# A feed-forward block's second product by sevens: operand loads apart from their splits, the residual in quarter pieces, the last product half by half

## The chip, the core and the metric

The kernel runs on one core of a Trainium2 chip. Times are microseconds of that core; the figure for a kernel is the median of its runs. Beside it stands one execution under the hardware profiler, from which every row below is taken. In the profile's names PE is TensorE's matmuls and PEld its weight loads, DVE is VectorE, ACT ScalarE, POOL GpSimd, and SP SyncE, the engine that issues nearly all DMAs here. L165 is line 165 of the kernel.

## What is computed

One layer of a decoder trunk on 1024 new tokens of a prompt and 8 x 8 sample tokens, all in fp32: a half-step feed-forward block, a token mixer (pooling branch and state-space branch), a second feed-forward block, a last norm. The change lies in the feed-forward block, which runs twice:

```python
def swiglu(x, w_in, w_out):
    gu = x @ w_in                                   # (tokens, 1024) @ (1024, 2 * 2816)
    g, u = gu[..., :D_FF], gu[..., D_FF:]
    return (jax.nn.silu(g) * u) @ w_out             # (tokens, 2816) @ (2816, 1024)

x = x + 0.5 * swiglu(rmsnorm(x, norm_ffn1), ffn1_w_in, ffn1_w_out)
x = x + mixer(rmsnorm(x, norm_mix), ...)
x = x + 0.5 * swiglu(rmsnorm(x, norm_ffn2), ffn2_w_in, ffn2_w_out)
y = rmsnorm(x, norm_final)
```

## The kernel before

**Layout.** Activations lie with channels on the 128 partitions and tokens along a row. The tokens are cut into two halves h of 512 and 576 (576 includes the 64 sample tokens); each half again into two token groups of NPAIR = 256 or 288, `f` and `s_` in the code. An fp32 matrix is multiplied as two parts, a rounded one and the rest: `split` (lines 354 to 360) makes the rounded part on ScalarE (L356) and the rest on VectorE (L358), and three matmuls take the place of one: weight part `wh` with operand parts `hh` and `hr`, weight part `wl` with `hh`. All matmuls are recorded at line 165, all transposes at 169.

**By sevens.** Both products of a feed-forward block use the scheme that multiplies 2 x 2 blocks with seven products instead of eight, from sums of blocks. In the first product (`ffn_in`, over 22 blocks `ff` of 128 hidden channels) `hidden(h, ff, g)` (L683) takes each finished block `g`. Blocks in pairs, even and odd, and the two token groups are the 2 x 2 blocks of the second product's operand: products 1, 2 and 3 use three of them as they are, 5, 6, 7 and 4 differences, which `sums` computes on POOL (L702). Each of the seven operands is stored by a DMA (L689) to DRAM as `hblock["1"]` to `["7"]`, 11 blocks of 128 x 544 each: 256 columns of half 0 and 288 of half 1.

**The second product** (`second`, L708) takes the seven in the order 1 2 5 6 4 7 3. A product has four *units* m, one for each 128 output channels of a half of the 1024; a unit has 11 steps k (in three chunks of 4, 4 and 3), each of three matmuls for each half: 66 matmuls, accumulated in PSUM banks `po`, one for each half (`unit`, L776). `weights` (L749) loads the raw weight block of a chunk (`raw`, L733, a ring of 6 tiles), for 5, 6 and 7 makes a sum or difference of two on POOL (L757, L761, L766; the sums of 5 are held in 12 tiles `ws`, turned into those of 6 in place and by `fourth`, L774, into those of 3), and `parts` (L739) makes `wh` on ScalarE (L745) and `wl` on VectorE (L746) in rings of 3 each. `leave` (L790) adds half of the unit's result to the output tiles on VectorE (L795).

- Operand blocks: `load_X(p)` (L719) loads one block and emits its split at once. Blocks 0 to 3 lie in 8 `pair` tiles (for product 1 in the pool `fx`), later ones in two tiles of the pool `act`, which has 42 and serves nearly everything. During a product the next one's first 8 blocks are loaded, 0, 3, 3 and 2 after its units (L839); the other three stand at the next product's start (L826).
- Residual: in product 7 each unit loads four whole tiles of the old x from DRAM (`xo`, L835) and after its `leave` adds them on POOL (L821, 512 or 576 columns each).
- The last product, 3: units 0 and 1 for both halves, then units 2 and 3 for half 0, `after(0)`, then units 2 and 3 for half 1, `after(1)`. What `after` starts is the norm that the next stage needs (the mixer, or the last norm with its transposes and the output).
- Before `second` the differences of all blocks, `hsums`, are finished (L671).

**Order.** Work is emitted in the order of the code, and side work (norms, differences, squares) as generators ("chains") that `tick` steps between groups of matmuls, when an estimate of TensorE's time has passed the step's due time: `H_AT` and `H_PACE` (L46) are that delay and pace for the differences. The tile framework then places the instructions of each engine's queue itself: the order of the code is their priority (`high_priority` lifts it), and an instruction goes as soon as the framework's own clock has its inputs ready and its tiles free. In the trace the first load of product 1 stands at 279.8 us, long ahead of `second`. On the chip each queue then runs strictly in the order made.

Of the kernel before, what the change touches and what calls it, by code (L numbers as in the profile page):

```python
# [8 lines left out]
F32 = mybir.dt.float32  # L9
# [5 lines left out]
P = 128  # L15
# [30 lines left out]
H_AT, H_PACE = 4.0, 1.5  # L46
# [17 lines left out]
def tile_hybrid_pool_ssd_macaron(  # L64
# [586 lines left out]
    def ffn(wi, wo, prep, after, half, side=None):  # L651
# [19 lines left out]
        while hsums:  # L671
            finish(hsums.pop(0))
# [10 lines left out]
    def hidden(h, ff, g):  # L683

        n, i, at = NPAIR[h], ff // 2, HALF_AT[h]
# [5 lines left out]
        if ff % 2 == 0:  # L691
            even[h] = g
            put("1", g[:, f])
            return
# [12 lines left out]

    def second(wo, after, half):  # L708
# [7 lines left out]
        xo = {}  # L716
        held = {}

        def load_X(p):  # L719
            k = len(X[p])  # L720
            if k >= 4:
                a, r = act((P, 576), F32R, "hh"), act((P, 576), name="hr")
            elif p == "1":
                a, r = fx(F32R, "hh"), fx(name="hr")
            else:
                a, r, _ = pair(576, "hp")
                r = r.bitcast(F32)
            a, r = a[:, :N2], r[:, :N2]
            dma(r, hblock[p][k])
            split(r, a, r.bitcast(F32R))  # L730
            X[p].append((a, r.bitcast(F32R)))
# [7 lines left out]
        def parts(a, nk, own):  # L739
            if own:  # L740
                wh, wl = (act((P, 4 * P), F32R, t)[:, : nk * P] for t in ("wh", "wl"))
            else:
                wh, wl = (sp.tile([P, 4 * P], F32R, tag=t, bufs=N_W, name=nm(t))[:, : nk * P] for t in ("wh", "wl"))
            with tc.high_priority(hp[0]):
                S.activation(wh, a, AF.Copy)  # L745
                V.tensor_tensor(wl, a, wh.bitcast(F32), op=ALU.subtract)  # L746
            return wh.rearrange("p (k c) -> p k c", c=P), wl.rearrange("p (k c) -> p k c", c=P)

        def weights(p, m, own=False):  # L749
            for kb, nk in chunks:  # L750
                if p in "124":
# [10 lines left out]
                elif p == "7":  # L762
# [4 lines left out]
                else:  # L767
                    a = held.pop((m, kb))
                yield (kb, nk) + parts(a, nk, own)
# [20 lines left out]
        def leave(p, m, h, pt):  # L790
# [20 lines left out]
            elif p == "6":  # L811
                add(a[:, s_], b[:, s_])
                add(b[:, f], t)
            elif p == "4":
                add(b[:, f], b[:, f])
            elif p == "7":
                add(b[:, f], b[:, f])
                add(b[:, s_], a[:, s_])
                for q in (4 + m, m):
                    o = xo.pop((h, q))  # L820
                    G.tensor_tensor(xt[h][q][:, : 2 * n], xt[h][q][:, : 2 * n], o, op=ALU.add)  # L821
            else:
                add(a[:, s_], a[:, s_])

        for p, nxt in zip(order, order[1:] + " "):
            while len(X[p]) < NK2:  # L826
                load_X(p)
            if p == "3":
                break
            for m in range(4):  # L830
                if p == "7":
                    for h in HALVES:
                        for q in (4 + m, m):
                            o = xo[h, q] = act((P, 576), name="xo")[:, : NTOK[h]]
                            dma(o, xspill[h][q])  # L835
# [16 lines left out]
        for h in HALVES:  # L852
            for m in (2, 3):
# [1075 lines left out]
```

## Time and profile before

| | us |
|---|---|
| median of 3 runs (2996.34 to 3004.19) | 2999.07 |
| the profiled execution, as timed | 2992.67 |
| its span in the profile | 2990.9 |
| mean granted clock of TensorE | 0.977 |
| matmuls of the second product, first block | 559.87 to 832.07 |
| matmuls of the second product, second block | 2699.36 to 2975.48 |

How to read it: the span runs from the first instruction to the last; 1.8 us of the timed execution lie around it. A row of the table of windows gives for a stretch of the span its length, the busy time and the instructions (x) of PE, PEld, DVE, ACT and POOL, the clock that TensorE was granted (1.00 is full), the mean busy share of the 16 DMA engines and GB/s. A row of a timeline gives start, length, engine, line, operation, the tile written and the tiles read (`<-`), and in brackets the idle time of the engine before it with what ended it. A row of a group gives the count, the busy time, the mean length in ns, then the idle time before its instructions and what ended it. "SPq" are issues of DMAs.

### The profile page before, as it was taken

To read this page: it belongs to the slowest core of one execution; us is meant where nothing else is said; L and a number is where in the kernel's file an instruction comes from. 1 tells how busy PE (TensorE), PEld (TensorE's weight loads), DVE (VectorE), ACT (ScalarE), POOL (GpSimd) and SP (SyncE) were. 2 spreads that over 40 slices of the span, in tenths; PEclk is the share of its full clock that TensorE was granted. 3 is DMA by queue.
4 is the path that set the end of the run, shared out by engine and by line. 5 is a ranking of instruction groups with operands and counts; after the bars stand their busy time and mean duration, and the time that the engine had idled before them with its cause. 6 is when DMAs were issued, how large, how long until landed. Compare 5 with 4: busy or idle time off the path is not lost. (4 is left out here: it accounts for less than half of the span.)

```text
span 2990.9 us, 54693 instructions
## 1 busy us (share of the span) xinstructions
PE 2813.4 (94%) x19834; PEld 2624.2 (88%) x19834; DVE 1859.9 (62%) x2848; ACT 1400.5 (47%) x3086; POOL 1345.7 (45%) x1392
## 2 busy tenths in 40 slices
PE   7889999999889999999998999898999999998987
PEld 6888899899869999999997887677999999988987
DVE  6655555666685376867675767866665555554746
ACT  5444443533344465555545656566233444344323
POOL 5645666343452264645632233323135665561533
PEclk9999999999999999999999999999999999999999
DMA  4566543576635545553357577786674332335773
GB/s 133 155 214 201 168 137 99 172 228 182 219 88 148 168 157 186 165 172 121 106 195 220 181 217 240 246 259 191 227 252 145 100 110 92 101 116 173 232 223 112
DMA packets 562255, 512.49 MB, mean 171 GB/s; under 512 B 39348, under 2 KB 426792, under 8 KB 561976
## 3 DMA queue, kind: packets, MB, share of 16 engines
q1 hardware_dynamic: 561968, 508.99, 54.4%
q8 instruction: 156, 2.56, 0.4%
q14 instruction: 115, 0.94, 0.1%
q10 hardware_dynamic: 16, 0.00, 0.0%
HBM read 361.28 MB, written 147.80 MB: 170 GB/s over the span
## 5 line engine op out<-in xcount | busy, mean ns | idle before, releaser
L165 PE MATMUL pw<-X,wh 128*128 128x288 f32 (+2 forms) x2832 | 632.2, 312 | 9.6 <-ACT v L565 8.3
L165 PEld LDWEIGHTS pw<-X,wh 128*128 128x128 f32 x2832 | 465.6, 191 | 32.9 <-ACT v L565 9.4
L165 PE MATMUL pw<-X,wl 128*128 128x288 f32 (+1 forms) x1644 | 475.8, 289 | 0.9 <-DVE wl L449 0.9
L449 DVE TENSOR_TENSOR wl<-s,wh 128x512 fp32r<-128x512 f32 x288 | 252.3, 876 | 282.0 <-ACT wh L448 260.9
L165 PE MATMUL pw<-hl,wh 128*128 128x256 f32 (+1 forms) x1536 | 392.0, 328 | 3.3 <-DVE t L569 3.0
L165 PE MATMUL pw<-hi,wh 128*128 128x288 f32 x1120 | 331.3, 296 | 2.6 <-ACT t L601 1.3
L165 PE MATMUL pw<-hi,wl 128*128 128x288 f32 x1120 | 330.2, 295 | 0.8 <-DVE wl L449 0.8
L165 PE MATMUL pw<-lo,wh 128*128 128x288 f32 x1120 | 329.7, 294 | 0.0
L442 POOL TENSOR_TENSOR s<-wraw,wraw 128x512 f32<-128x512 f32 x144 | 196.2, 1362 | 280.5 <-DVE wl L449 209.2
L165 PEld LDWEIGHTS pw<-X,wl 128*128 128x128 f32 x1644 | 314.1, 191 | 1.5 <-DVE wl L449 1.5
L165 PE MATMUL pw<-hl,wl 128*128 128x256 f32 x1072 | 300.3, 280 | 0.0
L165 PEld LDWEIGHTS pw<-hl,wh 128*128 128x128 f32 x1536 | 258.8, 189 | 24.4 <-DVE t L569 3.3
L448 ACT ACTIVATE wh<-s 128x512 fp32r<-128x512 f32 x288 | 181.0, 629 | 155.1 <-PE pw L165 130.6
L449 DVE TENSOR_TENSOR wl<-wraw,wh 128x512 fp32r<-128x512 f32 x216 | 174.9, 811 | 110.6 <-ACT wh L448 101.5
L165 PEld LDWEIGHTS pw<-hi,wh 128*128 128x128 f32 x1120 | 210.5, 188 | 9.8 <-ACT t L601 2.0
L165 PEld LDWEIGHTS pw<-hi,wl 128*128 128x128 f32 x1120 | 210.1, 188 | 1.4 <-DVE wl L449 1.3
L165 PEld LDWEIGHTS pw<-lo,wh 128*128 128x128 f32 x1120 | 210.6, 188 | 0.0
L165 PE MATMUL po<-hh,wh 128*128 128x256 f32 (+1 forms) x848 | 186.3, 296 | 20.2 <-ACT hh L356 10.2
L165 PEld LDWEIGHTS pw<-hl,wl 128*128 128x128 f32 x1072 | 203.0, 189 | 0.0
L448 ACT ACTIVATE wh<-wraw 128x512 fp32r<-128x512 f32 x216 | 135.5, 627 | 141.0 <-PE pw L165 121.5
L165 PE MATMUL po<-hh,wl 128*128 128x256 f32 (+1 forms) x848 | 185.4, 295 | 7.3 <-DVE wl L746 7.0
L165 PE MATMUL po<-hr,wh 128*128 128x256 f32 (+1 forms) x848 | 185.0, 295 | 1.1 <-DVE hr L358 1.0
(396 smaller groups left out, 6817.0 us busy)
## 6 DMA issues: line engine op xcount, KB each, us to landing
wraw<-in_ffn_w_in_dram SPq DMA_DIRECT2D x188, 256.0 KB
wraw<-in_ffn_w_out_dram SPq DMA_DIRECT2D x144, 256.0 KB
wraw<-in_w_in_dram SPq DMA_DIRECT2D x144, 256.0 KB
wh<-part SPq DMA_DIRECT2D x116, 256.0 KB
wl<-part SPq DMA_DIRECT2D x116, 256.0 KB
hr<-hb SPq DMA_DIRECT2D x106, 272.0 KB
hb<-g SPq DMA_DIRECT2D x154, 144.0 KB
hb<-g SPq DMA_DIRECT2D x154, 128.0 KB
```

Of the source, the lines that this page charges most:

```text
L165: T.matmul(out, lhsT, rhs, start=start, stop=stop, skip_group_check=free)
L442: G.tensor_tensor(t, a, b, op=op)
L448: S.activation(wh, a, AF.Copy)
L449: V.tensor_tensor(wl, a, wh.bitcast(F32), op=ALU.subtract)
```

## The change

- `H_AT, H_PACE` go from 4.0, 1.5 to 0.3, 0.3: the differences of a pair of blocks are emitted right behind it.
- `hidden` is cut in two. For the very last block, `hidden_odd` (stores of operands 2 and 3, differences, stores of 5, 6, 7, 4) is put in `hlast` for both halves; `second` first emits all loads and splits of operand 1, then these, then the rest of `hsums`.
- `load_X` becomes `fetch_X(p, n)`, which only issues n loads, and `split_X(below)`, which emits the splits of what has been fetched: at the last chunk of each unit of both halves, and (for blocks under 8) at a product's start. After each unit up to 3 blocks of the next product are fetched, until `AHEAD` of them are there: 11 of products 2 and 5, 8 of 6 and 4, 10 of 7 and 3; the others at the next product's start.
- Residual: of the output tiles' four quarters three are loaded by `old` in pieces of 256 and 288 columns (the first in product 6, two in 7) and added on POOL after the unit; the fourth is loaded by DMA straight into its place in product 6 and the sum that belongs there is added on POOL in product 4.
- Product 3 runs units 0 to 3 for half 0, `after(0)`, units 0 to 3 for half 1, `after(1)`. All 12 pairs of weight parts are kept from one half to the other: unit 0's in the rings `wh` and `wl`, unit 1's in the raw ring and `act`, those of 2 and 3 in `act` (15 tiles of it).

```diff
@@ -43,7 +43,8 @@
...
-H_AT, H_PACE = 4.0, 1.5
+H_AT, H_PACE = 0.3, 0.3
+AHEAD = {'2': 11, '5': 11, '6': 8, '4': 8, '7': 10, '3': 10}
...
@@ -668,8 +669,6 @@
                 ffn_in(wi, ff, [(h, X[h])])
         if side:
             finish(side)
-        while hsums:
-            finish(hsums.pop(0))
         second(wo, after, half)
...
     def hidden(h, ff, g):
 
+        if ff == NFF - 1:
+            hlast.append(lambda: hidden_odd(h, ff, g))
+        elif ff % 2:
+            hidden_odd(h, ff, g)
+        else:
+            even[h] = g
+            n, at = NPAIR[h], HALF_AT[h]
+            dma(hblock["1"][ff // 2][:, at : at + n], g[:, :n])
+
+    def hidden_odd(h, ff, g):
+
         n, i, at = NPAIR[h], ff // 2, HALF_AT[h]
         f, s_ = slice(0, n), slice(n, 2 * n)
 
         def put(p, x):
             dma(hblock[p][i][:, at : at + n], x)
 
-        if ff % 2 == 0:
-            even[h] = g
-            put("1", g[:, f])
-            return
         e = even[h]
         put("2", g[:, f])
         put("3", g[:, s_])
@@ -705,6 +711,8 @@
 
         hsums.append(start(sums(), H_AT))
...
+    hlast = []
+
     def second(wo, after, half):
...
+        raws, held, late_ = [], {}, []
+
+        def fetch_X(p, n):
+            for k in range(len(X[p]), min(len(X[p]) + n, NK2)):
+                if k >= 4:
+                    a, r = act((P, 576), F32R, "hh"), act((P, 576), name="hr")
+                elif p == "1":
+                    a, r = fx(F32R, "hh"), fx(name="hr")
+                else:
+                    a, r, _ = pair(576, "hp")
+                    r = r.bitcast(F32)
+                a, r = a[:, :N2], r[:, :N2]
+                dma(r, hblock[p][k])
+                raws.append((k, r, a))
+                X[p].append((a, r.bitcast(F32R)))
+
+        def split_X(below=NK2):
+            while raws and raws[0][0] < below:
+                _, r, a = raws.pop(0)
+                split(r, a, r.bitcast(F32R))
...
@@ -736,18 +748,26 @@
...
+        def ring(tag, nk):
+            n = {"wraw": N_RAW, "wh": N_W, "wl": N_W}[tag]
+            if tag == "wraw":
+                return sp.tile([P, 4 * P], F32, tag=tag, bufs=n, name=nm("wh")).bitcast(F32R)[:, : nk * P]
+            return sp.tile([P, 4 * P], F32R, tag=tag, bufs=n, name=nm(tag))[:, : nk * P]
+
...
-        def weights(p, m, own=False):
+        def weights(p, m):
             for kb, nk in chunks:
+                if p == "3":
+                    a = held.pop((m, kb))
+                    wh = act((P, 4 * P), F32R, "wh")[:, : nk * P] if m > 1 else ring(("wh", "wraw")[m], nk)
+                    wl = act((P, 4 * P), F32R, "wl")[:, : nk * P] if m else ring("wl", nk)
+                    yield (kb, nk) + parts(a, nk, wh, wl)
+                    continue
...
-                    a = held.pop((m, kb))
-                yield (kb, nk) + parts(a, nk, own)
+                yield (kb, nk) + parts(a, nk, ring("wh", nk), ring("wl", nk))
...
+        def old(m, q, col):
+            t = act((P, 576), name="xo")
+            for h in HALVES:
+                n, at = NPAIR[h], HALF_AT[h]
+                dma(t[:, at : at + n], xspill[h][4 * q + m][:, col * n : (col + 1) * n])
+
+            def put():
+                for h in HALVES:
+                    n, at = NPAIR[h], HALF_AT[h]
+                    o = xt[h][4 * q + m][:, col * n : (col + 1) * n]
+                    G.tensor_tensor(o, o, t[:, at : at + n], op=ALU.add)
+
+            late_.append(put)
+
         def unit(p, m, hs, ws):
             pts = [psum("pd", "po" + p)[:, : NPAIR[h]] for h in hs]
             for kb, nk, wh, wl in ws:
+                if kb == 8 and len(hs) == 2:
+                    split_X()
                 for kk in range(nk):
                     k = kb + kk
                     for j, (W_, lo_) in enumerate(((wh, 0), (wh, 1), (wl, 0))):
...
             elif p == "6":
                 add(a[:, s_], b[:, s_])
                 add(b[:, f], t)
+                dma(b[:, s_], xspill[h][4 + m][:, s_])
             elif p == "4":
                 add(b[:, f], b[:, f])
+                G.tensor_tensor(b[:, s_], b[:, s_], a[:, s_], op=ALU.add)
             elif p == "7":
                 add(b[:, f], b[:, f])
-                add(b[:, s_], a[:, s_])
-                for q in (4 + m, m):
-                    o = xo.pop((h, q))
-                    G.tensor_tensor(xt[h][q][:, : 2 * n], xt[h][q][:, : 2 * n], o, op=ALU.add)
+                add(b[:, s_], b[:, s_])
             else:
                 add(a[:, s_], a[:, s_])
...
-        for p, nxt in zip(order, order[1:] + " "):
-            while len(X[p]) < NK2:
-                load_X(p)
-            if p == "3":
-                break
+        fetch_X("1", NK2)
+        split_X()
+        while hlast:
+            hlast.pop(0)()
+        while hsums:
+            finish(hsums.pop(0))
+        for p, nxt in zip(order[:-1], order[1:]):
+            split_X(8)
+            fetch_X(p, NK2)
             for m in range(4):
-                if p == "7":
-                    for h in HALVES:
-                        for q in (4 + m, m):
-                            o = xo[h, q] = act((P, 576), name="xo")[:, : NTOK[h]]
-                            dma(o, xspill[h][q])
+                if p == "6":
+                    old(m, 0, 0)
+                elif p == "7":
+                    old(m, 1, 0)
+                    old(m, 0, 1)
                 unit(p, m, HALVES, weights(p, m))
                 if p == "4":
                     fourth(m)
-                for _ in range((0, 3, 3, 2)[m]):
-                    load_X(nxt)
+                while late_:
+                    late_.pop(0)()
+                n = AHEAD[nxt] - len(X[nxt])
+                fetch_X(nxt, min(n, 3))
+        fetch_X("3", NK2)
+        split_X()
         for h in HALVES:
             half(h, xt[h])
-        for m in (0, 1):
-            unit("3", m, HALVES, weights("3", m))
-        kept = {m: [] for m in (2, 3)}
+        kept = {m: [] for m in range(4)}
 
         def keep(m):
-            for w in weights("3", m, own=m == 3):
+            for w in weights("3", m):
                 kept[m].append(w)
                 yield w
 
         for h in HALVES:
-            for m in (2, 3):
+            for m in range(4):
                 unit("3", m, [h], kept[m] if h else keep(m))
             after(h, xt[h])
```

More of the change, by code (lines that the diff above doesn't have):

```diff
@@ L737, in raw, with parts @@
             return t
[L739 to L743, printed above, removed]
+        def ring(tag, nk):
[3 more added lines that the diff above has]
+            return sp.tile([P, 4 * P], F32R, tag=tag, bufs=n, name=nm(tag))[:, : nk * P]
+        def parts(a, nk, wh, wl):
             with tc.high_priority(hp[0]):
@@ L761, in weights @@
                         G.tensor_tensor(a, a, x, op=ALU.subtract)
-                elif p == "7":
+                else:
                     a = stage["p"].tile([P, 4 * P], F32, tag="wsum", bufs=N_S, name=nm("ws"))[:, : nk * P]
```

16 lines of the change are left out of this document (removed).

## The prediction

> **What bounds the kernel now.** I read the page first, for the share of TensorE, then the table of busy time by windows, with the edges set where the matmuls into `po` (line 165) change product: 66 matmuls are a unit, four units a product, in the order 1 2 5 6 4 7 3.
>
> ```profile
> span 2990.9 us, 54693 instructions
> PE 2813.4 (94%) x19834; PEld 2624.2 (88%) x19834; DVE 1859.9 (62%) x2848; ACT 1400.5 (47%) x3086; POOL 1345.7 (45%) x1392
> ```
>
> ```profile
> 559.87:599.80 39.93, 36.47 (x266) 35.20 (x265) 17.42 (x26) 15.93 (x32) 4.14 (x4) 0.91 0.58 174
> 599.80:639.04 39.24, 33.72 (x266) 33.06 (x264) 20.14 (x33) 16.71 (x30) 3.87 (x3) 1.00 0.69 206
> 639.04:673.63 34.59, 34.59 (x264) 34.59 (x265) 26.44 (x28) 12.85 (x22) 27.77 (x19) 0.95 0.91 260
> 673.63:709.33 35.70, 33.80 (x267) 33.15 (x265) 28.52 (x43) 14.45 (x26) 8.82 (x6) 1.00 0.58 172
> 709.33:745.75 36.42, 34.23 (x267) 33.31 (x265) 18.94 (x29) 10.13 (x18) 14.63 (x11) 1.00 0.64 186
> 745.75:791.25 45.50, 37.28 (x266) 35.38 (x265) 24.44 (x35) 11.20 (x20) 27.89 (x22) 0.92 0.87 277
> 791.25:832.07 40.82, 36.66 (x278) 35.98 (x276) 26.52 (x41) 16.90 (x30) 9.75 (x8) 0.96 0.44 137
> ```
>
> ```profile
> 2699.36:2739.57 40.21, 36.66 (x267) 35.38 (x266) 17.17 (x26) 15.70 (x31) 3.69 (x4) 0.92 0.56 172
> 2739.57:2780.60 41.03, 34.25 (x267) 33.14 (x265) 20.70 (x35) 16.64 (x30) 4.42 (x3) 0.98 0.63 195
> 2780.60:2816.09 35.49, 35.49 (x265) 35.49 (x266) 26.48 (x27) 12.80 (x22) 28.44 (x19) 0.92 0.89 259
> 2816.09:2851.45 35.36, 33.78 (x266) 33.15 (x265) 28.63 (x43) 14.39 (x26) 8.57 (x6) 1.00 0.57 171
> 2851.45:2886.39 34.94, 33.77 (x267) 33.21 (x265) 17.81 (x28) 10.13 (x18) 14.21 (x11) 1.00 0.66 197
> 2886.39:2931.21 44.82, 37.06 (x267) 35.39 (x265) 23.69 (x34) 11.09 (x20) 28.01 (x22) 0.92 0.79 244
> 2931.21:2975.48 44.27, 41.23 (x320) 40.54 (x319) 28.80 (x45) 19.11 (x44) 10.52 (x8) 0.96 0.10 32
> ```
>
> ```profile
> 2714.80:2739.57 24.77, 24.77 (x201) 24.77 (x200) 8.67 (x14) 9.28 (x20) 0.00 (x0) 1.00 0.37 112
> ```
>
> The columns are stretch, length, busy time of PE, PEld, DVE, ACT and POOL, granted clock, DMA share and GB/s. The last row is three units without a wait: 24.77 / 3 = 8.26 us a unit, 33.0 a product, 231.2 for seven. The two phases last 272.2 and 276.1 us, so 41 + 45 = 86 us are lost in them; this, and what follows the first phase, is all that the change can win. The losses by product: 1: 6.9 and 7.2; 2: 6.2 and 8.0; 5: 1.6 and 2.5; 6: 2.7 and 2.3; 4: 3.4 and 1.9; 7: 12.5 and 11.8; 3: 7.8 and 11.3 (part of it matmuls of others: 278 and 320 instead of 264). The view of the tile `po` says what ended its waits:
>
> ```profile
>   ACT wh L745: 44.9, 18
>   DVE wl L746: 33.9, 38
>   ACT hh L356: 22.6, 18
> ```
>
> So TensorE waits for ScalarE and VectorE, which are half idle. The timelines of ScalarE and SyncE at the start of product 7 show why:
>
> ```profile
> 2886.61 0.63 ACT L745 ACTIVATE wh<-ws 128x512 fp32r<-128x512 f32 x1 [1.93 <-POOL ws L766]
> 2895.78 0.66 ACT L356 ACTIVATE hp<-hp 128x544 fp32r<-128x544 f32 x1 [8.54 <-DMA hp<-hb]
> ```
>
> ```profile
> 2890.37 0.48 SPq L729 DMA_DIRECT2D hp<-hb  x1
> 2890.89 3.67 SPq L835 DMA_DIRECT2D xo<-xspill  x6
> 2894.68 1.41 SPq L729 DMA_DIRECT2D hp<-hb  x2
> ```
>
> ScalarE stands 8.54 us in front of the split of a block that the *next* product needs; that load and six residual loads share the queue. Behind it stand the weight parts that TensorE needs now. Queues are in order, so an early operand split blocks a late weight.
>
> **The change, part by part.** Each term is what of a loss goes.
>
> *Start of product 1 (14.1 lost).*
>
> ```profile
> 2701.11 0.80 SPq L689 DMA_DIRECT2D hb<-g  x2
> 2701.96 0.92 SPq L729 DMA_DIRECT2D hr<-hb  x2
> 2703.48 0.51 PE L165 MATMUL po<-hh,wh 128*128 128x256 f32 x2 [2.23 <-ACT hh L356]
> ```
>
> The two last loads of operand 1 stand on SP behind stores of the last hidden block, which wait for its product on POOL; TensorE then idles, and the product's granted clock is 0.91. The change emits all eleven loads and splits ahead of those stores (`hlast`); what is moved back, twelve stores on SP and eight subtractions on POOL a phase, is read 33 us later, by product 2 or after. Bounds 0 (the loads wait for their tiles anyway) to 14; I take 11, near the upper end, because the row names the store.
>
> *Products 2 and 5 (18.3 lost).*
>
> ```profile
> 2773.90 0.66 ACT L356 ACTIVATE hh<-hr 128x544 fp32r<-128x544 f32 x1 [2.92 <-DMA hr<-hb]
> 2779.93 1.55 ACT L745 ACTIVATE wh<-ws 128x512 fp32r<-128x512 f32 x3
> ```
>
> Splits of operand 5 and 6 come between 2773.90 and 2779.93, each behind its own DMA, and the first weights of product 5 after them. In the code of before each load past the fourth draws its tile after the tile of the split before it, so loads and splits take turns; now three loads go out together, a unit earlier, all eleven of operands 2 and 5 before their product, and the splits stand at the last chunk of the next unit, some 6 us behind. Bounds 0 to 17; I take 12, two thirds, because the six splits of the row's stretch do not vanish but only stop waiting.
>
> *Products 6 and 4 (10.3 lost).* Eight blocks ahead as before, the last three at the product's start. I take 3.5 (0 to 7), for the earlier unit. What they get in addition, a quarter of the residual each on POOL and 0.28 MB more loads a unit in product 6, goes beside a DMA share of 0.58 and 8.8 us of POOL in 35.7: nothing, and rival C if that cover fails.
>
> *Product 7 (24.3 lost).*
>
> ```profile
> 2904.42 5.64 POOL L821 TENSOR_TENSOR x<-x,xo 128x512 f32<-128x512 f32 x4 [8.55 <-DVE x L795]
> ```
>
> Four residual additions take 5.64 us of POOL a unit, after the unit's last matmul and ahead of the next unit's weight sums. By bytes (shapes of the code, four to an element) product 7 moves now 24 raw weight blocks (5.8 MB), some 11 operand blocks of 128 x 544 (3.1) and all the residual (16 loads, 4.5): 13.4 MB, less six raws that fit in their ring beforehand (1.5), at the row's 277 GB/s 43 us for 33 us of matmuls. That is the product's length; the DMA queue sets it, with POOL close behind. The change brings half of the residual during 6 and leaves the other half here: 5.8 + 2.8 + 2.2 - 1.5 = 9.3 MB, 34 us. POOL's additions of a unit fall from 5.64 us to four of half the size, 3.6 us (0.9 each, the row of L702 below), and only two of these wait for the unit. Bounds 5 (the ScalarE wait stays) to 22; I take 15.
>
> *Product 3 (19.1 lost).* POOL reaches it with less behind it, and ten of eleven blocks are fetched; I take 6. Half by half, the first four units need three weight parts in 3.9 us each (33 x 24.77/198 x 256/272) instead of 8.26:
>
> ```profile
> L795 DVE SCALAR_TENSOR_TENSOR x<-po,x 128x256 f32<-128x256 f32 (+1 forms) x80 | 31.6, 430 | 13.8 <-PE po L165 13.7
> L746 DVE TENSOR_TENSOR wl<-ws,wh 128x512 fp32r<-128x512 f32 (+1 forms) x96 | 92.1, 968 | 46.0 <-ACT wh L745 43.6 <-PE ptf L169 2.2
> L746 DVE TENSOR_TENSOR wl<-wraw,wh 128x512 fp32r<-128x512 f32 (+1 forms) x72 | 50.9, 711 | 30.9 <-ACT wh L745 30.4 <-PE po L165 0.4
> L702 POOL TENSOR_TENSOR g<-g 128x256 f32<-128x256 f32 (+1 forms) x88 | 78.4, 898 | 25.3 <-DVE g L627 16.1 <-DVE g L578 7.9 <-DMA hb<-g 0.8
> ```
>
> VectorE: 3 x 0.968 + 0.43 = 3.3 of 3.9 us; it fits barely. The fifteen kept parts and operand 3's fourteen tiles are 29 of the 42 of their pool; with the last norm's tiles that makes 44, so two of them wait a unit of 4.4 us, with no matmul behind them. I add 4 us for both phases (0 to 15).
>
> *End of the first phase.*
>
> ```profile
> 833.00:848.00 15.00, 10.64 (x38) 6.59 (x38) 15.00 (x17) 8.64 (x16) 12.54 (x11) 1.00 0.05 20
> 848.00:865.00 17.00, 11.74 (x36) 8.79 (x37) 11.06 (x22) 5.42 (x13) 8.32 (x8) 0.60 0.24 64
> ```
>
> The mixer's first matmuls follow the norm of half 0; VectorE is busy all 15 us. Idle 4.4 + 5.3, and 0.4 of 17 us to the clock, less what overlaps: about 14. Half 0 would end 4 x 4.4 = 17.5 us before the phase ends instead of 8.7. But four of its eight split tiles come free in the last unit only. I take 9 (0 to 14), since the norm of half 1 behind it starts when it did. The second phase's end is a chain behind half 1: nothing.
>
> *Costed at nothing.* The sums of operand blocks start earlier in the first product. In the POOL timeline six of them already stand ahead of a weight sum
>
> ```profile
> 2610.76 1.88 POOL L702 TENSOR_TENSOR g<-g,g 128x256 f32<-128x256 f32 x2 [0.66 <-DMA hb<-g]
> 2617.42 1.28 POOL L442 TENSOR_TENSOR s<-s,wraw 128x512 f32<-128x512 f32 x1
> ```
>
> and TensorE works through that stretch. Without that cover 0.9 us for each of 9 x 2 odd blocks, 16 us, would be lost. The quarter pieces raise the residual's issues from 16 to 32 a phase, at some 0.5 us of SP (the x6 row above: 0.61), spread over 66 us. Eight of them write straight into `x` and wait for VectorE's addition of the unit; behind them on SP stand the next raw weights, with six in flight. I add 4 us (0 to 10).
>
> Sum: 11 + 12 + 3.5 + 15 + 6 + 9 - 4 - 4 = 48.5. The profiled execution took 2992.67 us (span 2990.9): 2944. The three runs' median is 2999.07, so **2950 us** as a median.
>
> **Rivals.** *A. Nearly every wait goes*: the upper ends, 14 + 17 + 7 + 22 + 12 + 14 = 86, less 6: 2919. For it: the engines are half idle. Against it: loads still meet at product starts.
>
> *B. The loads go where the scheduler puts them anyway.* The code's place is a priority only: a load of operand 3 goes out at 2890.37, three units before its place in the code. If splits still stand ahead of weights, the middle terms go, and there remain 8 at the start, 6 in product 7 and 6 at the end: 2979.
>
> *C. Slower: VectorE and POOL exclude each other.*
>
> ```profile
> L358 DVE TENSOR_TENSOR hr<-hr,hh x106: 706/725/1941, 283.4 to 2937.9; 128x544 fp32r<-128x544 f32 x106
> ```
>
> A split takes 725 ns, and up to 1941. The part beside POOL's sums takes 968 ns against 711. If a VectorE operation had to wait out each POOL operation, the sum of both would bound a product: product 7 then needs POOL 12 x 1.3 + 16 x 0.9 = 30 and VectorE 12 x 0.71 + 16 x 0.43 + 10 splits x 0.73 = 23, 53 us, 8 more than now; product 6, 28.5 + 8.8 + 7.2 = 44.5, 9 more; product 4, 18.9 + 14.6 + 7.2 = 40.7, 5 more. That is +44 for both phases against 32 of the other terms and 4 + 4 added: 20 us slower, 3019. It decides from the point where the sum exceeds the product. Against it: product 5 carries 26.44 + 27.77 = 54.2 us in 34.59 with TensorE never idle. [...]
>
> **Chances.** Forecast (2930 to 2968) 0.48; A 0.14; B and what lies between it and the forecast 0.22, of which 0.15 faster and 0.07 within the uncertainty; C and like costs 0.16, of which 0.01 within. Range: 2918 (A) to 2992 (B with its 20 us of terms down to 7), leaving out most of C. A measurement of this kernel tells about 0.3% (9 us) from no change: faster 0.48 + 0.14 + 0.15 = 0.77, same 0.08, slower 0.15.
>
> **What would show it.** Right: products 1, 2, 5 at 33 to 35 us each; product 7 at 35 to 40; no ScalarE wait above 3 us for `hb` in front of a `wh`; residual additions of 0.9 us; the matmuls after the first phase without gaps over 1 us. Wrong: product 7 still above 43, or 6 and 4 above 37 with VectorE full (C); waits for `hb` as long as before (B); the first four units of product 3 above 5 us; new waits of `pw` for weight sums in the first product.

## The result and the profile after

| | before | changed |
|---|---|---|
| median of 5 runs, us | 2999.07 (2996.34 to 3004.19) | 2973.63 (2964.69 to 2980.84) |
| ratio to before, 95% interval | 1 | 0.9908 (0.9882 to 0.9934) |
| span of the profiled execution, us | 2990.9 | 2971.9 |
| matmuls of the second product, first block, us | 559.87 to 832.07 | 560.90 to 828.07 |
| between the two phases, us | 1867.3 | 1858.2 |
| matmuls of the second product, second block, us | 2699.36 to 2975.48 | 2686.27 to 2955.98 |

The changed kernel is 0.9% faster, some 25 us, about half of the 48.5 us forecast and inside the range. The profiled executions differ by 19.0 us: 5.0 and 6.4 us are won in the two phases and 9.1 between them, and 1.5 are lost in front of and behind these stretches.

The page of the changed kernel, its first lines:

```profile
span 2971.9 us, 54814 instructions
PE 2805.6 (94%) x19834; PEld 2622.8 (88%) x19834; DVE 1852.5 (62%) x2848; ACT 1396.8 (47%) x3086; POOL 1354.8 (46%) x1424
```

The table of windows of the changed kernel, edges again at a product's first matmul, products in the order 1 2 5 6 4 7 3, first and second block. Columns as before: length, busy time of PE, PEld, DVE, ACT, POOL, granted clock, DMA share, GB/s.

```profile
560.90:596.57 35.67, 34.03 (x267) 33.17 (x265) 19.63 (x28) 15.00 (x31) 5.42 (x5) 1.00 0.61 184
596.57:630.96 34.39, 33.80 (x266) 33.14 (x265) 17.54 (x29) 13.24 (x25) 5.30 (x4) 1.00 0.67 194
630.96:673.54 42.58, 35.49 (x266) 34.61 (x265) 22.61 (x29) 11.74 (x21) 29.82 (x22) 0.96 0.85 242
673.54:714.87 41.33, 36.11 (x266) 35.65 (x265) 27.12 (x41) 16.51 (x29) 17.44 (x16) 0.92 0.60 185
714.87:750.12 35.25, 33.88 (x267) 33.20 (x265) 23.31 (x32) 11.59 (x21) 18.24 (x15) 1.00 0.72 212
750.12:793.37 43.25, 36.63 (x267) 36.09 (x265) 31.38 (x43) 17.55 (x31) 26.55 (x23) 0.88 0.90 265
793.37:828.07 34.70, 34.70 (x279) 34.70 (x278) 24.80 (x41) 16.20 (x28) 7.98 (x9) 1.00 0.35 111
```

```profile
2686.27:2723.72 37.45, 35.10 (x266) 34.79 (x265) 20.88 (x30) 15.08 (x32) 5.47 (x5) 0.95 0.59 180
2723.72:2756.72 33.00, 33.00 (x266) 33.00 (x265) 16.73 (x26) 12.11 (x22) 6.92 (x5) 1.00 0.65 197
2756.72:2797.47 40.75, 35.69 (x267) 34.79 (x265) 23.65 (x29) 11.86 (x21) 28.19 (x22) 0.96 0.89 252
2797.47:2837.44 39.97, 35.54 (x267) 34.56 (x265) 30.12 (x44) 17.37 (x31) 17.22 (x16) 0.96 0.61 194
2837.44:2870.76 33.32, 33.32 (x267) 33.07 (x265) 19.16 (x30) 10.43 (x18) 17.52 (x14) 1.00 0.73 214
2870.76:2914.37 43.61, 35.81 (x266) 35.09 (x265) 28.19 (x39) 15.41 (x28) 26.78 (x23) 0.88 0.76 224
2914.37:2955.98 41.61, 40.65 (x320) 39.13 (x319) 20.81 (x40) 14.89 (x37) 2.62 (x4) 1.00 0.14 52
```

Length less 33.0 is a product's loss. In both phases together, by the terms of the prediction:

| term | loss before | loss after | gain | forecast |
|---|---|---|---|---|
| product 1 | 14.1 | 7.1 | 7.0 | 11 |
| products 2 and 5 | 18.3 | 18.7 | -0.4 | 12 |
| products 6 and 4 | 10.3 | 17.9 | -7.6 | 3.5 |
| product 7 | 24.3 | 20.9 | 3.4 | 15 |
| product 3 | 19.1 | 10.3 | 8.8 | 6 - 4 |
| entry of the mixer | | | 9.1 | 9 |
| SP's waits, and the rest | | | -1.5 | -4 |

(2 and 5 are one term because a wait ahead of the first matmul of 5 counts into the stretch of 2.) So products 1 and 3 and the end of the phase paid, and the middle, where 5, 6 and 7 begin, did not. From the view of the tile `po` of the changed kernel, two rows of what ended its waits:

```profile
  ACT wh L759: 70.3, 23
  ACT hh L357: 0.3, 1
```

The waits for the rounded operand part `hh` (22.6 us before) are gone but for 0.3 us; those for the weight part `wh` have grown from 44.9 to 70.3 us. The timeline of ScalarE at the start of product 6, whose first matmul stands at 673.54:

```profile
668.24 0.64 ACT L759 ACTIVATE wh<-ws 128x512 fp32r<-128x512 f32 x1 [3.75 <-PE po L166]
677.57 0.66 ACT L357 ACTIVATE hp<-hp 128x544 fp32r<-128x544 f32 x1 [8.69 <-DMA hp<-hb]
678.13 1.19 ACT L357 ACTIVATE hh<-hr 128x544 fp32r<-128x544 f32 x2
679.23 1.19 ACT L357 ACTIVATE hp<-hp 128x544 fp32r<-128x544 f32 x2
680.32 0.61 ACT L759 ACTIVATE wh<-ws 128x512 fp32r<-128x512 f32 x1
```

and that of SyncE:

```profile
668.51 4.61 SPq L748 DMA_DIRECT2D wraw<-in_ffn_w_out_dram  x4
673.17 1.92 SPq L736 DMA_DIRECT2D hp<-hb  x4
```

ScalarE stands 8.69 us in front of a block of operand 4, which the matmuls reach 37 us later, at 714.87. That block's load could go out only behind raw weights that wait for POOL (9.1 us between 655 and 675), and five splits pass before the second weight part of product 6, for which TensorE stands idle 4.28 us (its row is quoted at the end). In the code the load stands after unit 0 of product 6 and the split at the last chunk of unit 1. The framework put both one to two units earlier, as soon as tiles were free on its own clock.

### The profile page after: what moved, and what is told of

Same layout as the page of the kernel before. It is cut to its first block, busy times and chain, and to the rows that moved or that the text cites. A ratio compares the mean times of both kernels' runs of the same rounds, so it can differ in the third digit from the quotient of the medians.

```text
span 2971.9 us, 54814 instructions
## 1 busy us (share of the span) xinstructions
PE 2805.6 (94%) x19834; PEld 2622.8 (88%) x19834; DVE 1852.5 (62%) x2848; ACT 1396.8 (47%) x3086; POOL 1354.8 (46%) x1424
```

## The experiments

Each ratio is to the kernel before, run beside it on the same chip. The yardstick is the changed kernel, 0.9908 (0.9882 to 0.9934) and, once more,

**The changed kernel again.**

> The changed kernel once more, unaltered, as a yardstick for the runs beside it on one chip: 0.991 of the time of before (0.988 to 0.994), with the loss of products 5, 6 and 7 at 9, 8 and 10 us a phase again.

Measured: 0.9927 (0.9909 to 0.9945), 2971.89 us; losses of products 5, 6 and 7 in the two phases 10.8 and 12.7, 5.8 and 5.1, 10.0 and 10.9. The ratio and product 7 are as expected. Products 5 and 6 trade some us between executions, and their sum stays at 15 to 18 a phase.

**Theory 1: early splits in ScalarE's queue.** The rival is that POOL and the DMA queue pace these starts. In `split_X` and in `unit`:

```diff
...
+                if behind is not None:
+                    S.activation(a[:1, :1], behind[:1, 0, :1].bitcast(F32), AF.Copy)
                 split(r, a, r.bitcast(F32R))
...
                 if kb == 8 and len(hs) == 2:
-                    split_X()
+                    split_X(behind=wh)
```

> The changed kernel, with each operand split of a whole unit tied behind the weight part of the chunk at which the code writes it (a one-element ScalarE copy from `wh` into the split's output tile), so that the framework cannot put it earlier. The loads stay where they are. Theory 1 (the loss left at the starts of products 5, 6 and 7, 17.3 + 15.3 + 20.7 us in both phases, is ScalarE standing in front of splits of blocks 0 to 3 of the next operand, whose weights stand behind): these three fall to under 25 us together, ScalarE has no wait of over 3 us for `hb` ahead of a `wh` inside the phases, and the time is about 2945 us. Rival (these starts are paced by the weight sums on POOL and by the DMA queue, and the split only stands there while it waits): the same stretches keep 45 us or more, and the time lies within 5 us of 2973.6.

Measured: 0.9827 (0.9813 to 0.984), 2939.63 us against the yardstick's 0.9908 and 0.9927. Products 5, 6 and 7 of the held kernel, first block:

```profile
633.02:666.02 33.00, 33.00 (x266) 33.00 (x265) 26.05 (x30) 14.13 (x32) 23.93 (x17) 1.00 0.96 269
666.02:699.02 33.00, 33.00 (x266) 33.00 (x265) 29.56 (x38) 14.76 (x35) 25.87 (x22) 1.00 0.84 251
732.75:777.05 44.30, 36.90 (x264) 36.02 (x265) 30.72 (x40) 17.93 (x41) 28.77 (x25) 0.92 0.93 284
```

and ScalarE at the same place, where product 6 begins at 666.02:

```profile
666.02 0.53 ACT L761 ACTIVATE wh<-ws 128x384 fp32r<-128x384 f32 x1 [1.62 <-PE po L166]
666.58 0.39 ACT L744 ACTIVATE hh<-wh 1x1 fp32r<-1x1 f32 x3
666.87 1.74 ACT L357 ACTIVATE hh<-hr 128x544 fp32r<-128x544 f32 x3
669.02 0.63 ACT L761 ACTIVATE wh<-ws 128x512 fp32r<-128x512 f32 x1 [0.41 <-POOL ws L783]
```

Three splits now stand behind the third weight part of a unit, with their data there, and the next `wh` is not late. Products 1, 2, 5 and 6 lose 0.0 us in both phases, product 4 one us in both together; in product 7 there remain 11.3 and 11.2. What ended the waits of `po` in the held kernel, one row:

```profile
  ACT wh L761: 22.3, 11
```

70.3 us have become 22.3, and ScalarE, which waits 19 times for over 3 us for an operand block in the two phases of the changed kernel, does so not once here. Theory 1 is shown for the starts of 5 and 6: the same loads, sums and bytes pass without a wait. For 7 it is refuted: its loss did not fall (20.9 to 22.5), part of it only moved from the first unit to later ones. The two phases together lose 35.8 us instead of 74.9, but the span is only 31.8 us shorter: in this execution the second product of the first block begins 6.2 us later (567.08 instead of 560.90), behind a first product whose code the edit leaves as it is. The profiled executions of all forms begin it between 556 and 567.

**Is the hold enough by itself?** The kernel before, with the same one-element copy ahead of each split, from the last `wh` of the unit just written.

```diff
...
             dma(r, hblock[p][k])
+            if last:
+                S.activation(a[:1, :1], last[0][:1, 0, :1].bitcast(F32), AF.Copy)
             split(r, a, r.bitcast(F32R))
...
+            last[:] = [wh]
...
```

> The kernel before, with each operand split tied behind the last weight part of the unit after which the code writes it, by the same one-element ScalarE copy; nothing else of the change. Theory 1 (the waits are splits that stand ahead of weights in ScalarE's queue, whatever else is changed): the starts of products 1 to 6 come free also here, 20 to 35 us less: 2956 to 2970 beside 2991. Rival (it takes the loads of the change, three together and a unit earlier: here each load past the fourth waits for the tile of a split): within 8 us of the time of before.

Measured: 0.9986 (0.9974 to 0.9998), 2987.38 us. The time is the rival's, and theory 1's 20 to 35 us did not come. But the rival's reason is not borne out: products 2, 5, 6 and 4 come free also here, with 4.8 us lost in both phases instead of 28.6. What eats the gain is product 1, which loses 28.4 instead of 14.1, and product 7, 42.1 instead of 24.3; neither theory had that. Product 1's ScalarE and SyncE show where it waits:

```profile
569.41 0.66 ACT L356 ACTIVATE hh<-hr 128x544 fp32r<-128x544 f32 x1 [4.89 <-DMA hr<-hb]
```

```profile
564.02 2.43 SPq L689 DMA_DIRECT2D hb<-g  x3
566.50 0.42 SPq L730 DMA_DIRECT2D hr<-hb  x1
```

The last load of operand 1 stands behind three stores that wait for POOL, as the prediction said of the kernel before. In the changed kernel, with its loads of operand 1 in a row and its smaller residual, the hold pays; why products 1 and 7 lose more here than in the kernel before is not shown.

**Loads in a row, or in turns with the splits.**

```diff
-                raws.append((k, r, a))
+                split(r, a, r.bitcast(F32R))
```

> The changed kernel with each split written right behind its load again, so that loads and splits take turns; the numbers fetched ahead and all else stay. Theory J (the gain in products 1 and 2, 19 us in both phases, and the new loss at the starts of 5 and 6, 23 us, both come from the loads standing in a row apart from the splits): products 1 and 2 lose 10 us or more a phase again instead of 4, products 5 and 6 lose 4 to 8 a phase instead of 17, and the time is within 6 us of the changed kernel's 2972. Rival (the new loss is the residual loads of product 6 and the weight sums on POOL): 5 and 6 keep 14 us or more a phase, and the time is 2980 or more.

Measured: 0.9903 (0.9882 to 0.9925), 2963.51 us, no different from the yardstick. Products 1, 2, 5, 6, 4 lose 7.1, 0.9, 0.0, 3.5, 5.1 in the first block and 6.3, 0.2, 0.5, 5.0, 3.8 in the second. Products 1 and 5 of this kernel:

```profile
559.34:599.42 40.08, 36.41 (x267) 35.72 (x265) 18.56 (x28) 16.16 (x31) 4.08 (x4) 0.91 0.62 185
633.31:666.31 33.00, 33.00 (x266) 33.00 (x265) 20.66 (x28) 10.77 (x19) 24.76 (x19) 1.00 1.02 283
```

Theory J holds for product 1 (13.3 lost, near the 14.1 of before) and for product 5 (0.5 instead of 17.3), and the rival falls: 5 and 6 lose 3.5 and 5.5 a phase, with the residual loads and sums in place. It fails for product 2, which stays free, and for 6 and 4, which together lose 17.4 here and 17.9 in the changed kernel. So loads in a row win 6 us where the product cannot start without them, and lose as much or more where their splits come in a row in front of weights.

**The stores of the last hidden block first again.** `hidden` without `hlast`, and `hsums` finished ahead of `second`.

> The changed kernel with the stores and differences of the last hidden block in front of the loads of operand 1 again. Theory S (the stores ahead of those loads on the queue were the wait at the start of product 1): the first unit of product 1 goes back to 15 us in both phases and product 1 to about 40, the time is about 2981 us. Rival (the framework's own clock orders loads and stores the same way in both): product 1 stays under 38 us in both phases and the time within 4 us of 2973.6.

Measured: 0.9919 (0.9905 to 0.9933), 2966.08 us; product 1 loses 1.6 and 1.6 us. Theory S falls: with the loads in a row the last of them goes out at 560.4, ahead of the last five of those stores, in this form too. `hlast` was worth nothing that this can show.

**The pace of the differences.** `H_AT, H_PACE = 4.0, 1.5`.

> The changed kernel with the old delay and pace of the differences (4.0 and 1.5 instead of 0.3 and 0.3). Theory K (they are hidden behind the first product's matmuls in both kernels, as the prediction costed them): the second product begins within 2 us of 560.5 in the first block and the time is within 6 us of 2972. Rival (their earlier place is the gain in product 1, or costs the first product): product 1 goes back to 7 us of loss a phase, or the second product begins 5 us earlier or later.

Measured: 0.9913 (0.9895 to 0.9931), 2968.02 us; the second product begins at 560.44, product 1 loses 3.1 and 2.6. Theory K: nothing, as costed.

**Eight blocks ahead.** `AHEAD` 8 for all.

> The changed kernel with eight blocks of every operand fetched ahead and three at its product's start, instead of 11, 11, 8, 8, 10, 10. Theory L (product 3 gains from its ten blocks and product 2 from its eleven): product 2 loses 4 us or more a phase instead of 1, product 3 4 us more a phase, time about 2980. Rival (the framework hoists the last loads as far as their tiles let it in either form): both stay within 2 us, time within 5 us of 2972.

Measured: 0.993 (0.9916 to 0.9944), 2973.56 us; product 2 loses 0.0 and 1.7 (1.4 and 0.0 in the changed kernel), product 3 1.7 and 8.6, to the tenth as there. The rival holds: the numbers in `AHEAD` decide nothing here.

**Product 3 as it was.**

```diff
...
-        kept = {m: [] for m in range(4)}
+        for m in (0, 1):
+            unit("3", m, HALVES, weights("3", m))
+        kept = {m: [] for m in (2, 3)}
...
-            for m in range(4):
+            for m in (2, 3):
```

> The changed kernel with product 3 as it was (units 0 and 1 for both halves, then 2 and 3 half by half). Theory H (the 9.1 us won between the two phases are the norm of half 0 starting four units earlier): the stretch between the phases goes from 1858 back to 1867 us, product 3 changes by under 3 us a phase, and the time is about 2983 us. Rival (that time came from ten blocks of operand 3 being fetched ahead): the stretch stays at 1858 and the time within 4 us of 2973.6.

Measured: 0.9947 (0.9935 to 0.9959), 2973.21 us, by the ratios 0.2% to 0.4% above the yardstick (the kernel before ran at 2990.94 us beside it, so the times alone do not compare). The first 39 us behind the first phase, in the kernel before, the changed one and this one:

```profile
832.07:871.07 39.00, 28.45 (x102) 20.19 (x103) 33.02 (x48) 19.63 (x39) 22.38 (x21) 0.82 0.18 49
```

```profile
828.07:867.07 39.00, 33.41 (x135) 25.45 (x135) 33.21 (x58) 19.32 (x39) 18.26 (x19) 0.91 0.23 68
```

```profile
824.18:863.18 39.00, 28.37 (x105) 20.22 (x106) 33.02 (x48) 19.69 (x40) 22.29 (x21) 0.82 0.18 49
```

With half by half 135 matmuls pass instead of 102, and without it 105: the gain between the phases is the earlier norm. The 100th matmul behind the phase starts after 38.5, 28.9 and 37.7 us. Theory H holds here. The whole stretch went back by 6.5 us only (1858.2 to 1864.7); it differs by some us between executions of one kernel (1861.3 when the changed kernel ran again). All eleven profiled executions with half by half lie between 1852.5 and 1861.3, the three without it between 1864.7 and 1868.1. In product 3 the form costs 2.4 us: it loses 7.9 here instead of 10.3.

**The residual as it was**, four whole tiles a unit in product 7:

```diff
...
-                if p == "6":
-                    old(m, 0, 0)
-                elif p == "7":
-                    old(m, 1, 0)
-                    old(m, 0, 1)
+                if p == "7":
+                    for h in HALVES:
+                        for q in (4 + m, m):
+                            o = xo[h, q] = act((P, 576), name="xo")[:, : NTOK[h]]
+                            dma(o, xspill[h][q])
...
```

> The changed kernel with the residual as it was: four whole tiles a unit loaded and added in product 7. Theory R (the quarter pieces only shorten units 1 to 3 of product 7, which go from 29.5 to 24.8 us a phase; its first unit waits for splits): these units go back to 29 us, the rest stays, and the time is about 2982 us. Rival 1 (the residual set the whole product, 15 us as the prediction had it): product 7 grows by over 7 us a phase, time 2989 us or more. Rival 2 (the pieces loaded in product 6 delay its first unit): product 6 falls by 5 us a phase and the time stays at 2972.

Measured: 0.9984 (0.9974 to 0.9993), 2984.56 us: the pieces are worth 0.6% to 0.8%, 17 to 23 us, the largest part of the change. Products 7 and 3 of this kernel, first block:

```profile
743.64:792.29 48.65, 38.08 (x264) 36.48 (x265) 27.31 (x37) 14.68 (x26) 30.29 (x23) 0.89 0.85 263
792.29:833.20 40.91, 36.24 (x279) 35.02 (x278) 34.26 (x51) 19.48 (x34) 14.86 (x12) 1.00 0.37 115
```

Product 7 loses 30.6 in both phases instead of 20.9, and product 3 21.6 instead of 10.3; 2 and 5 lose 24.8 instead of 18.7, and 6 and 4 7.9 instead of 17.9. Theory R is right about product 7 (units 1 to 3 take 28.3 and 30.5 us instead of 24.8, and its first unit keeps its wait), but not in that the rest stays: half of the price stands in product 3, and so rival 1's time came, without its 7 us a phase in product 7. Rival 2 missed the time but is in part right at its place: product 6 loses 5.0 in both phases here, against 15.3 and 10.8 in the two executions of the changed kernel. Products 5 and 6 together fall by 4 to 6 us only (28.2 against 32.6 and 34.3), and the held kernel loads the same quarter in product 6 without a loss there; so in product 6 the quarter costs time only where splits stand in front of weights. The additions took 1046 ns in the median instead of 1607 (costed at 0.9 us):

```profile
L804 POOL TENSOR_TENSOR x<-x,xo x48: 723/1046/1302, 660.9 to 2916.5; 128x256 f32<-128x256 f32 x24, 128x288 f32<-128x288 f32 x24
```

```profile
L821 POOL TENSOR_TENSOR x<-x,xo x32: 1260/1607/1908, 764.4 to 2941.9; 128x512 f32<-128x512 f32 x16, 128x576 f32<-128x576 f32 x16
```

**What is left in product 7.** Three forms of the held kernel, with the residual quarters of product 7 taken elsewhere:

```diff
-                elif p == "7":
+                elif p == "4":
                     old(m, 0, 1)
+                elif p == "7":
+                    old(m, 1, 0)
```

> The kernel with held splits, with one of the two residual quarters of product 7 loaded and added in product 4 (1.1 MB of loads and 8 additions less a phase in 7). Theory D (the 11 us a phase left in product 7 are its DMA queue: raw weights, operand blocks and residual together): product 7's loss falls from 11 to 6 us a phase, product 4 stays under 1, about 2930 beside 2940. Rival (POOL's weight sums wait in POOL's own queue or for raw tiles): product 7 keeps 9 us or more a phase, time within 3 us of the held kernel.

Measured: 0.9796 (0.9779 to 0.9814), 2932.7 us; product 7 loses 10.9 and 9.7, product 4 0.0 and 0.4. One quarter less changed product 7 by 1 us a phase, as the rival had it. The time is near theory D's 2930, but by the profiled executions most of its gain on the held kernel stands outside the two phases: these lose 32.9 us instead of 35.8, and the second product begins 5.9 us earlier.

```diff
-                elif p == "7":
+                elif p == "4":
                     old(m, 1, 0)
                     old(m, 0, 1)
```

> As the run with one quarter moved, but both residual quarters of product 7 loaded and added in product 4. Theory D: product 7's loss falls to 2 us a phase, and product 4 takes up to 3 of it: about 2926. Rival: product 7 keeps 9 us or more a phase, or product 4 takes as much as 7 gives, time within 3 us of the held kernel.

Measured: 0.9768 (0.975 to 0.9786), 2925.36 us, the fastest kernel here. Products 4 and 7, first block, now with no residual in 7:

```profile
694.92:730.96 36.04, 33.17 (x267) 32.94 (x265) 27.48 (x33) 14.59 (x35) 28.01 (x26) 1.00 0.93 274
730.96:768.26 37.30, 35.35 (x264) 34.69 (x265) 25.09 (x40) 17.65 (x40) 15.81 (x14) 0.95 0.89 262
```

Product 7 loses 4.3 and 3.8 instead of 11, product 4 3.0 and 3.2: theory D's time (2926), though by a step and not in two equal parts.

**Two quarters in product 6, one in 4.**

> The kernel with held splits and no residual quarter left in product 7: two in product 6, one in 4. By the DMA theory product 6 has room for the second (its loss is 0 with one), so product 4 falls from 3 to under 1 us a phase, 7 stays at 4, 6 stays under 1, and the time is about 2921 beside 2925 of the form with two quarters in product 4. Rival (product 6 is as full as product 4): 6 loses what 4 gains, time within 2 us of 2925.

Measured: 0.9842 (0.9824 to 0.986), 2947.42 us, a miss for both theories. Products 4 and 7, first block:

```profile
699.22:739.52 40.30, 33.93 (x267) 33.09 (x265) 27.51 (x36) 14.91 (x36) 32.19 (x27) 1.00 0.75 227
739.52:782.21 42.69, 37.47 (x264) 36.42 (x265) 26.55 (x43) 19.63 (x44) 14.44 (x12) 0.92 0.86 256
```

Product 6 loses nothing, product 4 7.3 and product 7 9.7 with no residual in it at all. So a DMA queue that is too full in product 7 does not explain its loss alone. In product 4 POOL is busy 32.19 us against 28.01 in the form before. The author's reading, which no figure here shows, is that the additions left over from product 6 stand there ahead of the sums for product 3, which hold the raw tiles, and that ScalarE then waits for raw weights to land; no run separates this from the DMA queue, nor from the waits between VectorE and POOL shown under rival C below.

## Why the prediction was right, and where its steps failed

The side and the range were right, and the size was half of the forecast. Point by point:

- **What bounds the kernel** was right for the starts of the middle products: ScalarE in front of splits, with weights behind them. The held kernel changes the place of the splits, at the price of the small copies, and nothing else, and four products run without a wait. For product 7 it was not enough.
- **Product 1**: 7.0 instead of 11, for another reason than the step gives. Not the place of the twelve stores decides (undone: 3.2 us lost in both phases), but that the eleven loads go in a row (undone: 13.3). A load behind a store was a real wait (4.89 us in the kernel before with the hold), and the row of loads is what avoids it.
- **Products 2 and 5, 6 and 4**: this is the main step that failed. "The splits stand at the last chunk of the next unit, some 6 us behind" takes the place in the code for the place in the queue. The prediction's rival B had said that the place is a priority only; it came true for the middle products, with a cost that B did not have: in a row, a late load stops up to five splits, all of them ahead of the weights. Instead of +15.5 these terms gave -8.0. The residual quarter in product 6, costed at nothing "beside a DMA share of 0.58", goes with 6 to 10 us lost in product 6 by the run with the residual as it was, and with none where the splits are held.
- **Product 7**: 3.4 instead of 15 at its place. The residual pieces were worth 17 to 23 us, so the size was near and the place wrong: half of the gain stands in product 3, and product 7's first unit still waits for weights behind splits of the next operand (the 6.04 us quoted at the end). The step "the DMA queue sets it" failed too: by bytes the product was to take 34 us, and it took 43.25 and 43.61; with no residual in it, it took 37.30 us in one form and 42.69 in another.
- **Product 3**: 8.8 instead of 6 less 4. The 4 us for half by half were 2.4. Of the two reasons given for the 6, the blocks fetched ahead are none; the lighter residual on POOL is one (undone: 21.6 lost instead of 10.3).
- **End of the first phase**: 9 forecast, 9.1 between the phases and 9.6 at the 100th matmul, shown by undoing it.
- **Costed at nothing**: the pace of the differences, confirmed. The 4 us for SP's waits were not measured by themselves.
- **Its own signs of being wrong** came in part, though the time fell inside the range: product 7 stayed above 43, ScalarE's wait for an operand block in front of a `wh` is 8.69 us where the prediction's row had 8.54, product 5 took 42.58 and 40.75 us instead of 33 to 35, and two of the first four units of product 3 took 6.2 and 5.9 us in the second block (3.96 in the first).
- **Rival A** assumed that the change removes the waits; the held kernel, which does for products 1, 2, 5 and 6, reaches 0.9827, and with the residual of product 7 moved to product 4 0.9768, which is 2929 us by the ratio; A's 2919 was nearly there to be had.
- **Rival C**: its price did not come, but the prediction's argument against its mechanism fails. The busy time of an instruction in the trace can contain what it waits for the other engine (1.33 us for a split that alone takes 0.72, in the rows below), so 26.44 + 27.77 in 34.59 us, or 29.56 + 25.87 in 33.00 us in product 6 of the held kernel, does not speak against C; the price of C counted such waits too. Three rows of that product, the first of two additions in a row:

```profile
685.03 1.82 POOL L853 TENSOR_TENSOR x<-x,x 128x256 f32<-128x256 f32 x2
685.14 0.44 DVE L831 SCALAR_TENSOR_TENSOR x<-po,t 128x288 f32<-128x288 f32 x1
686.10 1.33 DVE L359 TENSOR_TENSOR hp<-hp 128x544 fp32r<-128x544 f32 x1
```

The split at 686.10 begins 0.75 us ahead of the end of POOL's addition (686.85) and ends 0.58 us behind it; alone a split takes 0.72 us, so this one all but stood still while POOL worked. The instruction at 685.14, which reads one of its two inputs from PSUM, takes 0.44 us beside the same additions. The 128 x 544 splits that begin at least 0.16 us ahead of the end of a POOL operation, 41 in the kernel before and 51 in the changed kernel, all finish 0.58 or 0.59 us behind it; 14 of the 41 stand in the two products 5 of the kernel before, where they take up to 1.82 us. So product 5 of the kernel before, which the prediction held against C, is no case against it. How much of product 7 this costs no run measures. An estimate, from the lengths that these instructions have alone in the trace (VectorE 0.69 us for 128 x 512, 0.72 for 128 x 544; POOL 1.29 for 128 x 512, 0.74 for 128 x 256), less 0.14 us each (0.72 less 0.58) for the start that may overlap: in the held kernel's first block they need some 29 us together in product 6 and some 33.5 in product 7, as long as its matmuls (33.0).

That the whole came to 25 us is thus: about 20 for the residual, 9 for the norm, 6 for product 1, less the 8 that products 2, 5, 6 and 4 lose more in sum under the new order of splits and the 2.4 that half by half costs in product 3. In the profiled executions three terms fell short by 39 us (product 1 by 4, the middle ones by 23.5, product 7 by 11.6), and 9 came back in product 3 and the rest; that the result lies inside the range owes more to its width (2918 to 2992) than to the sum. Single parts do not add up exactly, because a change to one product shows in another too: the residual as it was costs 9.7 us in product 7 and 11.3 in product 3.

Open stays what sets product 7's last 4 to 11 us: the DMA queue, POOL's queue, the ring of six raw tiles, or VectorE and POOL waiting for each other. The three forms do not tell them apart.

## What to carry to other kernels

Where a scheduler fills in-order queues, the place of an instruction in the code is a wish. If work for later must not stand in front of work for now, give it a true dependence on something that belongs to now: here 128 one-element copies of 0.19 us on an engine that is busy 48% of the span took away nearly all the waits of four of seven products. Look for a long wait on an engine's timeline, ask whether what it waits for is needed next, and read what stands behind it. And do not take two engines' busy times as proof that they work side by side: an instruction's length in the trace can contain a wait for the other engine, as in the 1.33 us of the split above.

## What the hardware showed besides

A wait of TensorE can cost more than its own length, some 3 us more in the first unit of product 6 by the rows below. Rows of the changed kernel, first the matmuls behind three waits with the idle time in brackets, then windows on the stretches of lowered clock around or behind them:

```profile
637.49 0.58 PE L166 MATMUL po<-hh,wh 128*128 128x256 f32 x1 [3.37 <-ACT wh L759]
```

```profile
680.98 0.38 PE L166 MATMUL po<-hh,wh 128*128 128x256 f32 x1 [4.28 <-ACT wh L759]
```

```profile
759.32 0.58 PE L166 MATMUL po<-hh,wh 128*128 128x256 f32 x1 [6.04 <-ACT wh L759]
```

```profile
681.59:688.42 6.83, 5.89 (x27) 5.71 (x26) 6.83 (x8) 4.08 (x7) 6.83 (x6) 0.50 0.95 291
756.69:766.93 10.24, 7.03 (x29) 6.71 (x30) 9.38 (x12) 5.92 (x10) 6.88 (x6) 0.50 1.14 328
637.22:640.63 3.41, 3.14 (x14) 3.14 (x15) 3.41 (x8) 2.80 (x6) 0.00 (x0) 0.50 1.12 323
```

The waits of 3.37, 4.28 and 6.04 us go with 3.41, 6.83 and 10.24 us at half the clock. But the length of a wait does not settle this. In the second block waits of 2.35, 2.70 and 3.93 us go with 3.41 us each; in the kernel before, 2.23 us (at 2703.48) goes with 6.83 and 4.25 us (at 639.04) with 3.41; and 3.30 us at 362.50 in the changed kernel goes with none. The first unit of product 6 takes 16.58 us instead of 8.25: waits of 4.28 and 0.94 us, and 6.83 us at half speed, of which TensorE works 5.89, so about 3 us are lost. The stretches are one, two and three times 3.41 us long, and the three above begin 44.37 and 75.10 us apart, which is 13 and 22 times 3.41. Whether it matters where on this spacing a wait falls, no run tests.
